# One small tile moved to another pool, two pads, and the result stored by halves in a two-layer PEER trunk

## The chip, the cores and the metric

The kernel runs on one core of one Trainium2 chip. Its engines are TensorE (PE in the rows; its weight loads are PEld), VectorE (DVE), ScalarE (ACT), GpSimd (POOL) and SyncE (SP), which issues most of the DMA transfers. The metric is the device time of one execution in microseconds (us), as the median of several runs.

## What is computed

The reference is a trunk of two layers over 512 tokens of 1024 channels, in float32. In each layer a mixing part is added to x and then a PEER part (product-key expert retrieval) is added. The PEER part matters most here:

```python
def peer_ffn(h, wq, keys, u, v):                      # u, v: 16384 experts x 1024
    q = (h @ wq).reshape(B, S, PEER_HEADS, 2, half)
    ...                                               # top 16 of the 16 x 16 best key pairs, 8 heads
    experts = e1 * PEER_NKEYS + e2
    gates = jax.nn.softmax(sc, axis=-1)
    def block(args):
        ht, et, gt = args
        act = jax.nn.gelu(jnp.einsum('td,ted->te', ht, u[et]), approximate=False)
        return jnp.einsum('te,ted->td', gt * act, v[et])
```

## The kernel before

The program is four parts one after the other: `mix_even`, `peer(0)`, `mix_odd`, `peer(1)`. Tokens are handled in four blocks of 128. In a PEER part block 0 gathers its experts' rows by indirect DMA (tile `gr`), and blocks 1 to 3 are computed densely over all 16384 experts, in 128 tiles of 128 experts.

**Split operands.** Each large float32 product is made of three fp32r matmuls: an operand is split into a high and a low part (`split`, L53 on ACT and L54 on DVE), and high x high, high x low and low x high are accumulated (`mm3`, L87 to L89; `v_sweep`, L1156). A weight tile comes by DMA as `raw` (four buffers) and is split into `whi` and `wlo` (three buffers each); these live in the pool `ws`. The transposed activations `hhi` and `hlo` live in the pool `hp`. In the rows a matmul reads `out<-moving,stationary`.

**The two stages of a PEER part.** The first stage (`u_step`, L87 to L89, `pu<-hhi,whi`) computes the activations of 128 experts for 384 tokens: stationary `whi`, moving `hhi`. The activation goes by way of `xact` to DRAM (`aside`), or stays in `act`. Meanwhile the gates of all experts are made (`big`, to DRAM as `G`). The second stage (`prepare` and `v_sweep`) loads gates (`gc`) and activations (`at`), multiplies them (L1096), splits the product into `wh` and `wl` (L1100, 128 x 384), and for each expert tile issues 18 matmuls of 512 columns (L1156, `acc<-whi,wh`): stationary a 128-column piece of `wh` or `wl`, moving a half of `whi` or `wlo`. Each stationary piece is used for two matmuls in a row, into two accumulators.

**Other matmuls of 512 columns.** `out_proj` (L221) is the output projection of both mixing parts, by the same lines: stationary the mixing result, moving `whi` and `wlo`. In `mix_even` the result lies in a `hhi`/`hlo` tile of the pool `hp`; in `mix_odd` it lies in `ohi` and `olo` of the pool `m1`. In `mix_odd` the first two weight tiles of the value projection are split into `vhi` and `vlo` of the pool `lead` (moving, against stationary `hhi`/`hlo`), the next two into `whi` and `wlo` by the same `sweep`. The forget gates use 16-column stationary pieces of `wfh` and `wfl` (`pf`, L685 to L687).

**Order.** The instructions are put in order by the framework's scheduler, engine by engine; SP issues its transfers in the program's order, each waiting for its own semaphores.

**Lines that the change touches.** `mix_even` (L291) allocates `gc0`, the first norm's gains, 128 x 8 float32, in the pool `np` for the whole program, and loads it ahead of the token blocks 1 to 3; `first_norm` reads it in L324 and L325. `np` lies before the pools of the parts, so all of these lie behind `gc0`. `odd_begin` (L635) opens `lead` on the right side of the memory; `mix_odd_body` (L659) has the tile `fb`; L1189 to L1192 add the accumulators to x; L1231 and L1232 store x.

Of the kernel before, what the change touches and what calls it, by code (L numbers as in the profile page):

```python
# [6 lines left out]
F32 = mybir.dt.float32  # L7
# [11 lines left out]
P = 128  # L19
D = 1024  # L20
T = 512
NB = T // P
KD = D // P
# [5 lines left out]
DB = (1, 2, 3)  # L29
# [18 lines left out]
class Trunk:  # L48
# [242 lines left out]
    def mix_even(self):  # L291
        nc, tc, A = self.nc, self.tc, self.A
        hT = self.new_hT()
        gc = self.np.tile([P, KD], F32, name="gc0")
        nc.sync.dma_start(gc, A["gain0"])
        for b in range(1, NB):
            nc.sync.dma_start(self.xb[b], A["x"][b * P:(b + 1) * P])

        self.early = [self.raw(A["w_in0"][i]) for i in (0, 4, 3, 7)]
        with tc.tile_pool(name="m0c", bufs=1) as sc:  # L300
            nc.sync.dma_start(self.cst[:, P:], A["consts"][:, P:])
            self.first_norm(gc, hT)
            self.mix_even_body(hT, sc)
# [331 lines left out]
    def odd_begin(self):  # L635


        nc, tc, A = self.nc, self.tc, self.A
        with tc.issue_after(self.last_gelu.ins), tc.issue_after(self.last_act.ins):
            nc.scalar.preload_act_table_set("natural_log_exp_and_others")  # L640
        hT = self.new_hT()
        norm = self.norm(2, NB)
        pool = tc.tile_pool(name="lead", bufs=2, side="right", reuse_waits="tile")
        start, rest = self.nat_parts(A["w_v1"][0], self.rows(hT), 2, eng=nc.gpsimd, pool=pool.__enter__())

        def close():
            pool.__exit__(None, None, None)
            norm[2]()

        self.odd = hT, rest, close  # L650
        return hT, norm, start
# [7 lines left out]
    def mix_odd_body(self, hT, sc, rest):  # L659
        nc, tc, A = self.nc, self.tc, self.A  # L660
        self.t2 = 4
        with tc.tile_pool(name="m1", bufs=1) as sp:
            pool = tc.tile_pool(name="m1b", bufs=2)
# [1 line left out]
            qkg = sc.tile([P, 2], F32, name="qkg")  # L665
            nc.sync.dma_start(qkg, A["qk_g"])
            nc.vector.tensor_scalar(qkg[:, 0:1], qkg[:, 0:1], 0.125, None, op0=ALU.mult)
            fb = sc.tile([16, 1], F32, name="fb")
            nc.sync.dma_start(fb, A["fgate_b"])
            nmask = sc.tile([P, P], BF16, name="nmask")  # L670
            nmf = sc.tile([P, P], F32, name="nmf")
# [263 lines left out]
    def peer_body(self, L, hT, h0, run, last, sp, sb):  # L935
        nc, tc, A = self.nc, self.tc, self.A
# [250 lines left out]
        for b in range(nd):  # L1187
            run(v_sweep, tail, b)
            for c in range(2):  # L1189
                xa = self.xb[DB[b]][:, c * 512:(c + 1) * 512]  # L1190
                with tc.issue_after(self.last_xs.ins) if L == 0 else nullcontext():
                    nc.vector.tensor_tensor(xa, xa, acc[b][c], op=ALU.add)  # L1192
            if L == 0:
                scale(DB[b])
                if b == 1:
                    run(put, 0, hN, True)
# [9 lines left out]
    def build(self, stop=4, first=0):  # L1206
        nc, tc, A = self.nc, self.tc, self.A
        with tc.tile_pool(name="const", bufs=1) as cp, tc.tile_pool(name="ws", bufs=1) as self.ws, \
                tc.tile_pool(name="hp", bufs=1) as self.hp, tc.tile_pool(name="np", bufs=1) as self.np, \
                tc.tile_pool(name="dp", bufs=2, space=DRAM) as self.dp, \  # L1210
                tc.tile_pool(name="ps", bufs=1, space=PSUM) as self.ps:
            self.nx = 0
            self.x0 = cp.tile([P, D], F32, name="x0")
            self.open_x()
            cst = cp.tile([P, 5 * P + T], F32, name="cst")
            nc.sync.dma_start(self.x0, A["x"][0:P])
            nc.sync.dma_start(cst[:, 0:P], A["consts"][:, 0:P])
            self.ident, self.iota, self.o512, self.o128, self.b64 = [cst[:, i * P:(i + 1) * P] for i in range(5)]
            self.tri = cst[:, 5 * P:]
            self.orow = A["consts"][0:1, 5 * P:]  # L1220
            sc = cp.tile([P, 2], F32, name="sc")
            self.last_gelu = self.last_act = nc.vector.memset(sc[:, 0:1], -0.5)
            nc.vector.memset(sc[:, 1:2], EPS)
            self.mhalf, self.epsc = sc[:, 0:1], sc[:, 1:2]
            self.steps = cp.tile([P, 2, TOPK, TOPK], BF16, name="steps")
            self.stf = cp.tile([P, 2, TOPK], F32, name="stf")
            self.cst, self.early = cst, []
            for i, f in enumerate((self.mix_even, lambda: self.peer(0), self.mix_odd, lambda: self.peer(1))):
                if first <= i < stop:
                    f()  # L1230
            for b in range(NB):  # L1231
                nc.sync.dma_start(self.out[b * P:(b + 1) * P], self.xb[b])  # L1232
            self.close_x()


# [79 lines left out]
```

## Time and profile before

| what | value |
|---|---|
| median of 3 runs (lowest to highest) | 3128.29 us (3126.55 to 3131.29) |
| profiled execution, its own time | 3129.1 us |
| its span | 3127.3 us |
| PE busy | 3090.1 us (99%) |
| DVE, ACT, POOL busy | 77%, 44%, 35% |
| moved by DMA | 786.63 MB, mean 252 GB/s |

The span is the time from the first to the last instruction; 1.8 us of the profiled execution lie around it. In the rows a matmul's own duration is modelled and overlaps the next one's, so a stream of matmuls is read by the starts, not by the durations.

### The profile page before, as it was taken

Reading aid. Unit: us, or ns where it says so; the run is one execution under the profiler, and the core shown is the slowest. Engines: PE = TensorE matmul, PEld = TensorE weight load, DVE = VectorE, ACT = ScalarE, POOL = GpSimd, SP = SyncE. Lnnn points to the kernel's source line nnn. Section 1 sums busy time; section 2 is a strip of 40 time slices with the busy share of each in tenths; the row PEclk is TensorE's granted clock in tenths of the full one; section 3 lists DMA queues with packets and bytes.
Section 4 is the critical chain, followed back from the end, with each engine's and each line's share of the span. In section 5 each row is a group of like instructions: output and inputs, shape, how many; then the busy total and the mean of one; then the engine's idle time right before and its main releaser. Section 6 shows DMA issues by size and latency. Waiting matters only on the chain.

```text
span 3127.3 us, 45688 instructions
## 1 busy us (share of the span) xinstructions
PE 3090.1 (99%) x15932; PEld 2682.5 (86%) x15932; DVE 2403.1 (77%) x4938; ACT 1385.3 (44%) x2222; POOL 1102.7 (35%) x800
## 2 busy tenths in 40 slices
PE   8999999999999999999999999999999999999999
PEld 6668999999999888888776669999999998888887
DVE  7765988888886888888646549998888867888886
ACT  4353334666664333333334433336666643333332
POOL 1210123996773222222100001219867742222220
PEclk9999999999999999999999999999999999999999
DMA  4103445999998999999421124449999998999995
GB/s 156 54 29 129 144 135 181 354 356 342 340 322 303 316 345 359 356 345 368 163 69 41 43 96 137 139 144 339 366 335 343 326 333 277 350 350 352 364 352 208
DMA packets 334201, 786.63 MB, mean 252 GB/s; under 512 B 26873, under 2 KB 181898, under 8 KB 327826
## 3 DMA queue, kind: packets, MB, share of 16 engines
q1 hardware_dynamic: 260242, 515.24, 47.2%
q0 software_dynamic: 73728, 268.47, 24.5%
q8 instruction: 125, 2.05, 0.3%
q14 instruction: 106, 0.87, 0.1%
HBM read 687.07 MB, written 96.47 MB: 251 GB/s over the span
## 4 chain that ended last, share of the span: by engine, by line
PE 91%; DMA 3%; DVE 3%; issue 1%; ACT 1%; POOL 1%; SPq 0%; DVEq 0%; POOLq 0%; ACTq 0%
PE acc L1156 34%; PE pu L87 10%; PE pu L88 10%; PE pu L89 10%; PE bank L87 5%; PE bank L88 5%; PE bank L89 5%; PE bank L1030 4%; DMA gr<-in_uN_dram,ids 3%; PE pc L376 1%; PE po L779 1%; PE bank L747 1%; PE bank L1058 1%; DVE wlo L54 1%; DVE gr L982 1%
## 5 line engine op out<-in xcount | busy, mean ns | idle before, releaser
L53 ACT ACTIVATE whi<-raw 128x1024 fp32r<-128x1024 f32 x602 | 637.2, 1059 | 1531.4 <-issue 666.1
L54 DVE TENSOR_TENSOR wlo<-raw,whi 128x1024 fp32r<-128x1024 f32 x565 | 693.3, 1227 | 362.0 <-ACT whi L53 361.2
L87 PE MATMUL pu<-hhi,whi 128*128 128x384 f32 x2048 | 699.7, 342 | 0.9 <-ACT hhi L122 0.9
L89 PE MATMUL pu<-hhi,wlo 128*128 128x384 f32 x2048 | 688.1, 336 | 2.2 <-DVE wlo L54 2.2
L88 PE MATMUL pu<-hlo,whi 128*128 128x384 f32 x2048 | 686.0, 335 | 0.3 <-DVE hlo L123 0.3
L991 POOL DMA_INDIRECT gr<-in_vF_dram,ids x256 | 275.6, 1076 | 749.2 <-DVE x L993 724.6
L1156 PE MATMUL acc<-whi,wh 128*128 128x512 f32 x1536 | 450.5, 396 | 0.0
L1156 PE MATMUL acc<-wlo,wh 128*128 128x512 f32 x1536 | 449.8, 395 | 0.0
L1156 PE MATMUL acc<-whi,wl 128*128 128x512 f32 x1536 | 448.2, 395 | 0.0
L980 POOL DMA_INDIRECT gr<-in_uN_dram,ids x256 | 350.9, 1371 | 245.4 <-DVE dots L982 149.2
L87 PEld LDWEIGHTS pu<-hhi,whi 128*128 128x128 f32 x2048 | 385.6, 188 | 2.6 <-ACT hhi L122 1.3
L89 PEld LDWEIGHTS pu<-hhi,wlo 128*128 128x128 f32 x2048 | 384.8, 188 | 3.0 <-DVE wlo L54 2.8
L88 PEld LDWEIGHTS pu<-hlo,whi 128*128 128x128 f32 x2048 | 385.4, 188 | 2.3 <-DVE hlo L123 1.0
L1156 PEld LDWEIGHTS acc<-whi,wl 128*128 128x128 f32 x1536 | 288.6, 188 | 69.9
L1156 PEld LDWEIGHTS acc<-wlo,wh 128*128 128x128 f32 x1536 | 288.6, 188 | 69.6
L1156 PEld LDWEIGHTS acc<-whi,wh 128*128 128x128 f32 x1536 | 288.5, 188 | 69.4
L1020 POOL TENSOR_SCALAR a<-cst,sT 128x128 f32<-128x128 f32 x192 | 326.6, 1701 | 14.4 <-PE bank L1030 8.6
L993 DVE SCALAR_TENSOR_TENSOR x<-gr,dots,x 128x1024 f32<-128x1024 f32 x256 | 327.4, 1279 | 0.0
L982 DVE CUSTOM_DVE_ANT_0 gr<-gr,h 128x1024 f32<-128x1024 f32 x256 | 308.3, 1223 | 24.2 <-DMA gr<-in_uN_dram,ids 24.1
L1017 DVE TENSOR_TENSOR a<-cst,sT 128x512 f32<-128x512 f32 x192 | 132.7, 691 | 126.6 <-PE bank L1030 121.4
L54 POOL TENSOR_TENSOR wlo<-raw,whi 128x1024 fp32r<-128x1024 f32 x37 | 93.9, 2538 | 374.5 <-ACT whi L53 366.5
L87 PE MATMUL bank<-hhi,whi 128*128 128x512 f32 x512 | 211.0, 413 | 1.5 <-ACT hhi L122 1.5
(267 smaller groups left out, 4093.0 us busy)
## 6 DMA issues: line engine op xcount, KB each, us to landing
raw<-in_uT_dram SPq DMA_DIRECT2D x256, 512.0 KB
raw<-in_vF_dram SPq DMA_DIRECT2D x256, 512.0 KB
G<-big SPq DMA_DIRECT2D x48, 1024.0 KB
gc<-G SPq DMA_DIRECT2D x32, 1536.0 KB
aside<-xact SPq DMA_DIRECT2D x208, 192.0 KB
at<-aside SPq DMA_DIRECT2D x104, 384.0 KB
raw<-in_w_in_dram SPq DMA_DIRECT2D x32, 512.0 KB
raw<-in_wq_dram SPq DMA_DIRECT2D x32, 512.0 KB
```

What stands on the lines that cost most here:

```text
L53: first = self.nc.scalar.activation(hi, raw, AF.Copy)
L54: self.last_lo = (eng or self.nc.vector).tensor_tensor(lo, raw, hi.bitcast(F32), op=ALU.subtract)
L87: mm(out, lh, rh, start=first, stop=False)
L88: mm(out, lh, rl, start=False, stop=False)
L89: return mm(out, ll, rh, start=False, stop=last)
L980: nc.gpsimd.indirect_dma_start(out=r, out_offset=None, in_=uN, in_offset=bass.IndirectOffsetOnAxis(ap=ids[:, s:s + 1], axis=0))
L982: return lambda: nc.vector.tensor_tensor_reduce(r, r, h0, 1.0, 0.0, ALU.mult, ALU.add, accum_out=dots[:, s:s + 1])
L991: nc.gpsimd.indirect_dma_start(out=r, out_offset=None, in_=vF, in_offset=bass.IndirectOffsetOnAxis(ap=ids[:, s:s + 1], axis=0))
L993: return lambda: nc.vector.scalar_tensor_tensor(self.x0, r, dots[:, s:s + 1], self.x0, op0=ALU.mult, op1=ALU.add)
L1017: nc.vector.tensor_tensor(a2, self.iota[:, None, :].to_broadcast([P, 4, P]), e2[:, :, None].to_broadcast([P, 4, P]), op=ALU.is_equal)
L1020: (nc.vector if t else nc.gpsimd).tensor_scalar(a1[:, t], self.iota, e1[:, t:t + 1], gate[:, t:t + 1], op0=ALU.is_equal, op1=ALU.mult)
L1156: mm = nc.tensor.matmul(acc[b][c], wt[:, s], vt[:, c], start=(n == 0 and wt is wh and vt is vh), stop=(n == NE1 - 1 and wt is wl))
```

## The change

The first norm's gains `gc0` become a tile of the pool `m0c`, which lives only as long as the first mixing part, and their load is written behind the loads of the token blocks. With `gc0` out of `np`, everything that is allocated behind `np` starts 32 bytes lower in each partition; inside the first mixing part `gc0` takes these 32 bytes again, so the tiles there stay where they were. Two pads move two places further: a tile of 64 bytes in `lead`, and `fb`, which grows from 4 to 96 bytes. At the end each half of a block is stored behind its own addition, as six transfers of 128 x 512, instead of three of 128 x 1024; block 0 keeps its store.

```diff
@@ mix_even
-        gc = self.np.tile([P, KD], F32, name="gc0")
-        nc.sync.dma_start(gc, A["gain0"])
         for b in range(1, NB):
             nc.sync.dma_start(self.xb[b], A["x"][b * P:(b + 1) * P])
-        self.early = [self.raw(A["w_in0"][i]) for i in (0, 4, 3, 7)]
         with tc.tile_pool(name="m0c", bufs=1) as sc:
+            gc = sc.tile([P, KD], F32, name="gc0")
+            nc.sync.dma_start(gc, A["gain0"])
+            self.early = [self.raw(A["w_in0"][i]) for i in (0, 4, 3, 7)]
@@ odd_begin
-        start, rest = self.nat_parts(A["w_v1"][0], self.rows(hT), 2, eng=nc.gpsimd, pool=pool.__enter__())
+        lead = pool.__enter__()
+        start, rest = self.nat_parts(A["w_v1"][0], self.rows(hT), 2, eng=nc.gpsimd, pool=lead)
+        lead.tile([P, 16], F32, name="pad", bufs=1)
@@ mix_odd_body
-            fb = sc.tile([16, 1], F32, name="fb")
+            fb = sc.tile([16, 24], F32, name="fb")[:, 0:1]
@@ peer_body
                     nc.vector.tensor_tensor(xa, xa, acc[b][c], op=ALU.add)
+                if L:
+                    nc.sync.dma_start(self.out[DB[b] * P:(DB[b] + 1) * P, c * 512:(c + 1) * 512], xa)
@@ build
-            for b in range(NB):
-                nc.sync.dma_start(self.out[b * P:(b + 1) * P], self.xb[b])
+            nc.sync.dma_start(self.out[0:P], self.x0)
```

Where the tiles start in a partition, by the two built programs (bytes; the remainder is by 256; the buffers of one tile name lie multiples of 256 bytes apart, and so do the pieces of them that the matmuls use, except in `wfh`):

| tile | before | remainder | changed | remainder |
|---|---|---|---|---|
| `whi`, `wlo` (first buffers) | 42784, 55072 | 32 | 42784, 55072 | 32 |
| `hhi`, `hlo` | 67360, 83744 | 32 | 67360, 83744 | 32 |
| `wh`, `wl` | 163904, 168512 | 64 | 163872, 168480 | 32 |
| `ohi`, `olo` | 127872, 144256 | 128 | 127904, 144288 | 160 |
| `vhi`, `vlo` | 184288, 192480 | 224 | 184224, 192416 | 160 |
| `wfh`, piece k at + 64 k | 106112 | 128 (k = 0) | 106144 | 160 (k = 0) |
| `gc`, `at`, `xact`, `act0`, `h0` | 173120, 197696, 159296, 122432, 104512 | 64 | 32 bytes lower | 32 |
| `raw`, `gr`, `upad`, `x0` | | | unchanged | |

On PE, DVE, ACT and POOL every instruction stands where it stood. On SP two places differ. The first is the program's start: `x_72` is token block 0, `x` blocks 1 to 3, `gc_87` and `gc_93` are the gains, `raw` the first weight tiles. Before:

```order
L1216 DMA x_72<-in_x_dram 128x1024
L1217 DMA cst<-in_consts_dram 128x128
L295 DMA gc_87<-in_gain_dram 128x8
L297 DMA x<-in_x_dram 128x1024 x3
L59 DMA raw<-in_w_in_dram 128x1024 x4
```

and changed:

```order
L1220 DMA x_72<-in_x_dram 128x1024
L1221 DMA cst<-in_consts_dram 128x128
L295 DMA x<-in_x_dram 128x1024 x3
L298 DMA gc_93<-in_gain_dram 128x8
L59 DMA raw<-in_w_in_dram 128x1024 x4
```

The load of the gains has moved behind three loads of 512 KB. The second place is SP's end, the last weight tiles and the stores, before:

```order
L1000 DMA x<-kept 128x1024 x3
L1085 DMA at<-aside 128x2x384
L1232 DMA out_dram<-x_72 128x1024
L59 DMA raw<-in_vF_dram 128x1024 x3
L1232 DMA out_dram<-x 128x1024 x3
```

and changed:

```order
L1002 DMA x<-kept 128x1024 x3
L1087 DMA at<-aside 128x2x384
L1235 DMA out_dram<-x_72 128x1024
L59 DMA raw<-in_vF_dram 128x1024 x3
L1196 DMA out_dram<-x 128x512 x6
```

Three stores of 512 KB have become six of 256 KB; nothing stands behind them on SP.

## Rows read from the trace of the kernel before

**Rows 1.** The page's head and PE's row: busy, share, instructions.
```profile
span 3127.3 us, 45688 instructions
...
PE 3090.1 (99%) x15932; PEld 2682.5 (86%) x15932; DVE 2403.1 (77%) x4938; ACT 1385.3 (44%) x2222; POOL 1102.7 (35%) x800
```
**Rows 2.** Chain of work, second PEER stages (first cut at 1500): start, us, what.
```profile
1005.21 494.89 PE acc L1156 x2121
...
2586.66 535.74 PE acc L1156 x2296
```
**Rows 3.** Group of L1156: xcount | busy, mean ns; group of L87: xcount, ns min/median/max.
```profile
L1156 PE MATMUL acc<-whi,wh 128*128 128x512 f32 x1536 | 450.5, 396 | 0.0
...
L87 PE MATMUL bank<-whi,ohi x64: 391/398/790, 1783.0 to 1854.1; 128*128 128x512 f32 x64
```
**Rows 4.** Timeline of PE, output projection of mix_even: start, us, operation.
```profile
237.83 0.39 PE L87 MATMUL bank<-whi,hhi 128*128 128x512 f32 x1
...
245.99 0.39 PE L87 MATMUL bank<-whi,hhi 128*128 128x512 f32 x1
```
**Rows 5.** Timeline of PE, output projection of mix_odd.
```profile
1838.34 0.40 PE L89 MATMUL bank<-whi,olo 128*128 128x512 f32 x1
...
1847.47 0.39 PE L89 MATMUL bank<-whi,olo 128*128 128x512 f32 x1
```
**Rows 6.** Timeline of PE, value projection of mix_odd, two kinds of weight tile.
```profile
1556.71 0.39 PE L89 MATMUL bank<-vhi,hlo 128*128 128x512 f32 x1
...
1558.81 0.40 PE L89 MATMUL bank<-vhi,hlo 128*128 128x512 f32 x1
...
1564.33 0.39 PE L87 MATMUL bank<-whi,hhi 128*128 128x512 f32 x1
...
1565.92 0.39 PE L88 MATMUL bank<-wlo,hhi 128*128 128x512 f32 x1
```
**Rows 7.** Timeline of PE, forget gates, starts of pieces k = 1, 2, 3, 6, 7.
```profile
1559.50 0.40 PE L87 MATMUL bank<-hhi,wfh 128*16 128x512 f32 x1
...
1560.20 0.39 PE L87 MATMUL bank<-hhi,wfh 128*16 128x512 f32 x1
...
1560.88 0.40 PE L87 MATMUL bank<-hhi,wfh 128*16 128x512 f32 x1
...
1562.96 0.39 PE L87 MATMUL bank<-hhi,wfh 128*16 128x512 f32 x1
...
1563.64 0.40 PE L87 MATMUL bank<-hhi,wfh 128*16 128x512 f32 x1
```
**Rows 8.** Stretches: PE, PEld, DVE, ACT, POOL busy (x), PEclk, DMA share, GB/s.
```profile
1000.00:1500.00 500.00, 500.00 (x2150) 403.32 (x2150) 408.32 (x484) 177.71 (x242) 130.21 (x123) 1.00 0.97 339
...
1100.00:1108.40 8.40, 8.40 (x37) 6.76 (x36) 7.56 (x11) 2.95 (x4) 3.56 (x3) 1.00 1.08 351
1108.40:1116.80 8.40, 8.40 (x37) 6.76 (x36) 6.98 (x9) 2.95 (x4) 2.12 (x3) 1.00 1.03 402
```
**Rows 9.** Line L384, taps of the convolution: ns min/median/max.
```profile
L384 DVE SCALAR_TENSOR_TENSOR y<-upad,cw,y x79: 730/743/1779, 34.9 to 120.9; 128x512 f32<-128x512 f32 x79
```
**Rows 10.** Timeline of the program's start, SP's queue and ACT.
```profile
1.64 0.43 SPq L295 DMA_DIRECT2D gc<-in_gain_dram  x1
...
12.21 1.06 ACT L53 ACTIVATE whi<-raw 128x1024 fp32r<-128x1024 f32 x1 [0.23 <-DMA raw<-in_w_in_dram]
```
**Rows 11.** Stretches at the program's end, columns as in rows 8.
```profile
3124.00:3125.00 1.00, 0.00 (x0) 0.00 (x0) 0.00 (x0) 0.00 (x0) 0.00 (x0) 1.00 0.47 188
3125.00:3126.00 1.00, 0.00 (x0) 0.00 (x0) 0.00 (x0) 0.00 (x0) 0.00 (x0) 1.00 0.84 336
```
**Rows 12.** Timeline of PE, a query projection of peer(1) right after first-stage matmuls.
```profile
1867.36 0.39 PE L88 MATMUL bank<-hlo,whi 128*128 128x512 f32 x1
...
1869.21 0.39 PE L87 MATMUL bank<-hhi,whi 128*128 128x512 f32 x1
...
1877.60 0.39 PE L89 MATMUL bank<-hhi,wlo 128*128 128x512 f32 x1
```

## The prediction

> **What bounds the kernel now.** I began with the page's head and the busy line [rows 1]: PE is busy 3090.1 of 3127.3 us. At most some 37 us lie in PE's idle time; a larger gain must come from PE's own stream running faster, and what is saved on another engine is lost unless PE waited for it. The chain of waits, in order of time, says where nothing but PE decides: the second stage of each PEER part is one single piece, 2121 matmuls in 494.89 us in the first (cut at 1500) and 2296 in 535.74 us in the second [rows 2]. No wait is left inside them, and both make 233.3 ns per matmul. The groups by form give their number: three groups of 1536, so 4608 [rows 3], 1075 us or 34% of the span. The mean of one in that view (396 ns) is no guide, since matmuls overlap; the starts are.
>
> So I compared the starts of the same matmul (128 x 128 stationary, 512 columns moving, fp32r) in other places of the timeline:
> - Output projection of `mix_even`: 36 starts in 8.16 us, 226.7 ns each [rows 4].
> - Output projection of `mix_odd`, the same lines of code: 39 starts in 9.13 us, 234.1 ns [rows 5].
> - Value projection of `mix_odd` with moving `vhi`/`vlo`: 9 starts in 2.10 us, 233.3 ns; some 6 us later, the same loop with moving `whi`/`wlo`: 7 starts in 1.59 us, 227.1 ns [rows 6].
>
> There are two spacings, about 7 ns apart, for one shape. The same code runs at both, so it isn't the instruction pattern alone. What goes along with the spacing is the place of the operands, in the table of start addresses: where stationary and moving both leave 32 by 256, the matmuls start 226.7 ns apart; where one of them leaves 64 (`wh`), 128 (`ohi`) or 224 (`vhi`) against 32, they start 233.3 to 234.1 apart. That the remainder by 256 counts, and nothing longer, I take from the forget gates, whose stationary pieces step by 64 bytes: the three matmuls of k = 1 (remainder 192) take 0.70 us, those of k = 2 and of k = 6, which lie 256 bytes apart and both leave 0, take 0.68 [rows 7]. Rows are rounded to 0.01, so this is weak support, and there 0 does as well as 32. The trace doesn't show why the place should count.
>
> **The change part by part.**
>
> *Place of `wh` and `wl`.* They go from remainder 64 to 32, the remainder of the moving `whi` and `wlo`, the pairing of rows 4. I take 226.7 ns for all of them: 4608 x (233.3 - 226.7) = **30.7 us off**, all of it on the path, since the two pieces of rows 2 hold no wait. Ends of the range: 0 (they stay at 233.3) and 30.7 (no row of this shape is faster in a steady stream).
>
> *Cover for that.* The second stage of 1000 to 1500 must then be fed in 486 us instead of 500. DVE is busy 408 us of it, so it keeps 78 us; ACT and POOL are far off [rows 8]. DMA is nearest: 339 GB/s at a busy share of 0.97, which would have to be 349. One stretch of 8.4 us moves 402, its neighbour, at a share of 1.08, only 351 [rows 8]. Since the rate reaches 402 and the mean needed is 349, I cost this at nothing; without that cover it is the second rival. The Trainium skill ("DMA: Bandwidth & Descriptors", section "Where 436 GB/s comes from") puts the HBM limit of a core at about 358 GB/s; the stretch at 402 is above it, so the trace doesn't bear it out as a ceiling, and by it the stage would still fit, with little to spare.
>
> *Place of `ohi`/`olo` and `vhi`/`vlo`.* From 128 and 224 to 160, against 32. No row shows a 128-column tile at 160. Three groups of 64 matmuls on the projection [rows 3] at 234.1 could fall to 226.7 (1.4 us), 48 on `vhi` and `vlo` (two tiles, two halves, four blocks, three products) from 233.3 likewise (0.3 us). I take half, **0.8 off**, ends 0 and 1.7: 160 is 128 beyond 32, and half a period may or may not do.
>
> *All other shifted tiles* (`gc`, `at`, `act`, `h0` and so on, from 64 to 32; in `mix_odd` up by 32). DVE doesn't mind: 79 taps read `upad` at 31 different 4-byte offsets, minimum 730, median 743 ns [rows 9]. Zero; and what DVE would lose lies under PE, by the 78 us above. The first stages' matmuls use `whi`, `wlo`, `hhi` and `hlo` alone, which don't move: zero.
>
> *The gains' load.* Three token loads are issued 0.43 us earlier, the gains behind them [rows 10]. The first norm could be up to 0.43 us earlier; but ACT's split of the second weight tile at 12.21 waits for its own transfer [rows 10], whose issue doesn't move, and the first use of the gains stands behind it on ACT. **0.1 off**, ends 0 and 0.43. The gains' 4 KB arrive behind three loads of 512 KB; if they were later than that split, the first projection would wait for them.
>
> *The stores.* The last store of 512 KB fills 3124 to 3126: 188 and 336 GB/s for one us each [rows 11]. With 256 KB left behind the last addition, at 336 GB/s, 0.78 us less remain at most; the first half goes out during the second addition. **0.6 off**, ends 0 and 0.78. On SP only other stores stand behind, and no engine waits for them.
>
> The sum, against the profiled execution's own 3129.1 us (span 3127.3 and 1.8 around it): 3129.1 - 30.7 - 0.8 - 0.1 - 0.6 = 3096.9. That execution is 0.8 above the median of the runs, 3128.3; against the median it is **3096.1 us**, 1.0% faster.
>
> **The rivals.**
>
> *The spacing stays.* For it: the second stage has a pattern that no row shows at 226.7, each stationary piece used twice running, two moving halves into two accumulators. And the spacing is a state that a stream settles into rather than a fixed price: a query projection with all operands at 32 begins with 8 starts in 1.85 us, 231 ns each, and goes on with 37 in 8.39, 226.8 ns [rows 12]; the second stage never settled in 2296. Against it: rows 4 to 6, where the same code changes its spacing with the place. It leaves 0.1 to 1.5 us of gain: 3127.5. The Trainium skill ("SBUF — State Buffer", section "A bandwidth-pool intuition that's wrong (but worth ruling out)") gives TensorE a second, independent read port for weight loads and knows contention only where engines share a port; by it the place of the stationary operand could not matter, and the time would be this rival's. Rows 4 and 5 speak against it.
>
> *DMA takes over.* The stage runs at 226.7 until the gate loads, at 351 GB/s, hold back the weight tiles; half of the gain is given back: 3096 + 15 = 3111 or so. For it: the share of 1.08; against it: 402 GB/s right behind.
>
> *Slower: a worse pairing.* The second stages settle at a spacing above 233.3, since the place counts and the new pairing is not what I take it for. `ohi` at 234.1 shows that pairings differ upwards too. Each ns costs 4.6 us, so it is slower beyond 0.2% from 1.4 ns (6.3 us) up; one step of 6.7 ns more would give 3128 + 31 = 3159. Against it: no steady row of this shape above 234.1, and `wh` joins a pairing that rows 4 show.
>
> **How the numbers follow.** About 0.2% (6.3 us) is what a measurement of this kernel can tell from no change: 3122 to 3134.6 is the same. Chances: forecast 0.76, DMA 0.08, spacing stays 0.12, worse pairing 0.04. The first two are both faster: 0.84; same 0.12; slower 0.04. The forecast's own range: 3092 (0 for nothing, all ends at their far side, and 2 us for runs, which lie within -1.7 and +3.0 of their median) to 3101 (place of `ohi` and the stores worth nothing, beginnings at 231 ns, and 3 us for runs). With the DMA case it reaches to 3113; that holds a little over 0.8.
>
> **What would show it.** The two pieces of the chain: 2296 matmuls in about 520.5 us instead of 535.7, starts 226.7 ns apart; if they stay at 233.3, the reading of rows 4 to 6 is wrong, or right for those patterns only. First stages and first mixing part: unchanged lengths. `mix_odd`: starts of `ohi` at 226.7 or 234. The second stage's DMA near 349 GB/s and no PE idle time inside; gaps that end on `raw` would show the DMA case. The last transfers about 0.6 us shorter behind the last addition. Wrong altogether would be a change of time with the spacing unchanged.

## The result and the profile after

The changed kernel takes 3100.15 us (median of 4 runs, 3098.18 to 3100.8), the kernel before 3129.34 beside it (4 runs, 3126.55 to 3131.29): a ratio of 0.9906, 95% interval 0.9889 to 0.9923. It is faster, and the time lies in the range of the prediction (3092 to 3113), 4 us above the forecast of 3096.1. In a second series it took 3097.95 (4 runs), ratio 0.9905 (0.9888 to 0.9922). The profiled execution after has 3100.8 us of its own and a span of 3099.0; the one before had 3129.1 and 3127.3.

The page's head and the busy line, which answer to [rows 1]:

```profile
span 3099.0 us, 45694 instructions
...
PE 3058.8 (99%) x15932; PEld 2681.2 (87%) x15932; DVE 2401.9 (78%) x4938; ACT 1386.9 (45%) x2222; POOL 1109.5 (36%) x800
```

PE has the same 15932 matmuls and is busy 31.3 us less; the span is only 28.3 us shorter. So PE's stream runs faster, as forecast, and 3.0 us of PE's idle time have been added (40.2 us instead of 37.2). Both are followed below.

The chain of waits of after, the pieces of the second stages (start, us, what), which answer to [rows 2]; the first one here is not cut at 1500:

```profile
1005.23 505.89 PE acc L1158 x2232
...
2573.83 520.48 PE acc L1158 x2296
```

L1158 is L1156 of before. The second piece makes 520.48 / 2296 = 226.7 ns per matmul instead of 233.3, and 520.5 us were forecast. The first makes 505.89 / 2232 = 226.7; the same piece of before, uncut, is

```profile
1005.21 520.68 PE acc L1156 x2232
```

The two pieces are 14.79 and 15.26 us shorter, 30.05 together, and they still hold no wait. The stretch 1000 to 1500 of after, columns as in [rows 8]:

```profile
1000.00:1500.00 500.00, 500.00 (x2213) 414.60 (x2212) 416.46 (x494) 182.75 (x248) 132.34 (x123) 1.00 0.98 346
```

PE does 2213 matmuls in it instead of 2150, is never idle, and the DMA moves 346 GB/s (349 were forecast) at a share of 0.98. The rival in which the DMA takes over did not come. The granted clock is 1.00 in both kernels, the 2.4 GHz level; the spacing is no matter of the clock.

### The profile page after: what moved, and what is told of

The parts are those of the page before. It is cut to its first block, busy times and chain, and to the rows that moved or that the text cites. A ratio compares the mean times of both kernels' runs of the same rounds, so it can differ in the third digit from the quotient of the medians.

```text
span 3099.0 us, 45694 instructions
## 1 busy us (share of the span) xinstructions
PE 3058.8 (99%) x15932; PEld 2681.2 (87%) x15932; DVE 2401.9 (78%) x4938; ACT 1386.9 (45%) x2222; POOL 1109.5 (36%) x800
## 4 chain that ended last, share of the span: by engine, by line
PE 91%; DVE 3%; DMA 2%; issue 2%; ACT 1%; POOL 1%; SPq 0%; DVEq 0%; POOLq 0%; ACTq 0%
PE acc L1158 33%; PE pu L88 10%; PE pu L87 10%; PE pu L89 10%; PE bank L87 6%; PE bank L89 5%; PE bank L88 5%; PE bank L1032 4%; DMA gr<-in_uN_dram,ids 2%; PE pc L376 1%; PE po L781 1%; PE bank L749 1%; PE bank L1060 1%; DVE gr L984 1%; DVE wlo L54 1%
## 5 line engine op out<-in xcount | busy, mean ns | idle before, releaser
L87 PE MATMUL pu<-hhi,whi 128*128 128x384 f32 x2048 | 698.7, 341 | 1.2 <-ACT hhi L122 1.2
L1158 PE MATMUL acc<-whi,wh 128*128 128x512 f32 x1536 | 439.9, 389 | 0.0
L1158 PE MATMUL acc<-wlo,wh 128*128 128x512 f32 x1536 | 439.2, 389 | 0.0
L1158 PE MATMUL acc<-whi,wl 128*128 128x512 f32 x1536 | 437.3, 389 | 0.0
L87 PEld LDWEIGHTS pu<-hhi,whi 128*128 128x128 f32 x2048 | 385.7, 188 | 2.7 <-ACT hhi L122 1.4
L1158 PEld LDWEIGHTS acc<-whi,wl 128*128 128x128 f32 x1536 | 288.3, 188 | 59.9
L1158 PEld LDWEIGHTS acc<-wlo,wh 128*128 128x128 f32 x1536 | 288.3, 188 | 59.9
L1158 PEld LDWEIGHTS acc<-whi,wh 128*128 128x128 f32 x1536 | 288.2, 188 | 59.5
L1022 POOL TENSOR_SCALAR a<-cst,sT 128x128 f32<-128x128 f32 x192 | 334.6, 1743 | 14.3 <-PE bank L1032 6.3
L87 PE MATMUL bank<-hhi,whi 128*128 128x512 f32 x512 | 211.0, 413 | 1.4 <-ACT hhi L122 1.4
```

Source lines behind the costliest of these rows:

```text
L87: mm(out, lh, rh, start=first, stop=False)
L1022: (nc.vector if t else nc.gpsimd).tensor_scalar(a1[:, t], self.iota, e1[:, t:t + 1], gate[:, t:t + 1], op0=ALU.is_equal, op1=ALU.mult)
L1158: mm = nc.tensor.matmul(acc[b][c], wt[:, s], vt[:, c], start=(n == 0 and wt is wh and vt is vh), stop=(n == NE1 - 1 and wt is wl))
```

## The experiments

### Only the place of wh and wl

The kernel before with a pad of 224 bytes, and nothing else of the change:

```diff
                 wb, vb = wpool.__enter__(), vpool.__enter__()
+                wb.tile([P, 56], F32, name="pad", bufs=1)
```

> The kernel before with one edit: a 224-byte pad ahead of wh and wl, which brings them (and gc and at) to remainder 32 by 256; the gains' load, ohi, vhi, the first stages' tiles and the stores stay as before. Theory (the place of wh against whi alone makes the gain): both second stages at 226.7 ns per matmul (2296 in about 520.5 us), time about 30 us below before, near 3098 to 3099; ohi stays at 234.1, the program's start and the second layer's first stage are as in before, so it is 0 to 4 us faster than the changed kernel if the later start and the 3 us lost in that first stage come from the other edits. Rival (the gain needs the other moved tiles, as act, gc0 or the pools behind np): 233.3 ns stay, 3128. If the 3 us in the first stage are noise, this kernel shows them or not as it likes; if they come from the moved a1 and a2 tiles, the stage ends as in before.

Measured: 3099.8 us (4 runs), ratio 0.9906 (0.9889 to 0.9922), the same as the whole change. Its chain of waits, second layer:

```profile
2574.19 520.48 PE acc L1157 x2296
```

The same 520.48 us. The gain needs this one place and none of the other edits. The 0 to 4 us by which this kernel was to be faster than the changed one did not come: in the same series the changed kernel took 3097.95.

### The place of wh and wl taken back

The changed kernel with a pad of 32 bytes, which brings them back to 64:

```diff
                 wb, vb = wpool.__enter__(), vpool.__enter__()
+                wb.tile([P, 8], F32, name="pad", bufs=1)
```

> The changed kernel with a pad of 32 bytes ahead of wh and wl: they are back at remainder 64, all else of the change stays. Theory (place of wh against whi): second stages back at 233.3 ns, 2296 in 535.7 us, about 3130. Rival (the other tiles that moved bring the gain, or the stores do): 226.7 ns, 3100.

Measured: 3126.68 us (one run). Its chain, second layer:

```profile
2584.44 535.74 PE acc L1159 x2296
```

That is the 535.74 us of [rows 2], with all other edits in place. Together with the run before, the gain is undone and done by the place of these two tiles alone.

### Everything at 64

The changed kernel with 32 bytes ahead of the constants, so that the whole left side of the memory moves, `whi` and `wlo` with `wh` and `wl`:

```diff
+            cp.tile([P, 8], F32, name="pad")
             cst = cp.tile([P, 5 * P + T], F32, name="cst")
```

> The changed kernel with everything that lies on the memory's left side 32 bytes higher: whi, wlo, hhi, hlo, wh and wl all leave 64 by 256 (ohi 192, vhi stays at 160). Theory (what counts is that both operands leave the same remainder): second stages at 226.7 ns, as in the changed kernel, 3098 to 3100. Rival (the place of wh itself counts: 64 is a bad place for a stationary operand, or for any): 233.3 ns, about 3129, and the first stages and projections, now at 64 too, slow down with it.

Measured: 3095.27 us (one run). Its chain, second layer:

```profile
2568.28 520.48 PE acc L1158 x2296
```

Both operands at 64: 226.7 ns. Against `whi` at 32 the same 64 gave 233.3. So 64 is not a bad place by itself; it is the distance between the two that counts. The pads of the two runs before moved the tiles `gc` and `at` together with `wh`; here these two lie at 64 as in the kernel before, so they have no part in the gain.

### The other distances

Three kernels with another pad at the same place, a different one in each layer:

```diff
                 wb, vb = wpool.__enter__(), vpool.__enter__()
+                wb.tile([P, (56, 24)[L]], F32, name="pad", bufs=1)
```

The pads are 56 and 24 words for remainders 0 and 128, 16 and 32 for 96 and 160, 40 and 48 for 192 and 224.

> The changed kernel with wh and wl at remainder 0 in the first layer and 128 in the second, against whi at 32. Theory in its strict form (same remainder by 256 or slow): 233.3 ns in both stages, about 3129. Rival (remainder by 64 or 128 decides, or small distances are as good): 0 is 32 away as 64 is, so 233.3; 128 is 96 away; a stage that shows 226.7 falls out of the strict form.

> The changed kernel with wh and wl at remainder 96 in the first layer and 160 in the second. Theory in its strict form (same remainder by 256): 233.3 ns in both, about 3129. Rivals: a period of 64 gives 226.7 in both, 3099; a period of 128 gives 226.7 in the second alone, about 3114 (15 us of the 30 kept).

> The changed kernel with wh and wl at remainder 192 in the first layer and 224 in the second. Theory in its strict form: 233.3 ns in both, about 3129. Rival with a period of 64: 224 gives 226.7, 192 does not, about 3114. A third value of the spacing in a stage would say that the distance sets it step by step.

Measured: 3130.51, 3122.69 and 3119.94 us (one run each). Chain of waits, first layer (cut at 1500) and second layer, for remainders 0 and 128:

```profile
1005.21 494.90 PE acc L1159 x2121
...
2586.03 537.93 PE acc L1159 x2296
```

for 96 and 160:

```profile
1004.95 495.13 PE acc L1159 x2122
...
2582.63 533.56 PE acc L1159 x2296
```

and for 192 and 224:

```profile
1004.92 495.13 PE acc L1159 x2122
...
2587.90 525.54 PE acc L1159 x2296
```

Length by count, with `whi` and `wlo` at 32:

| `wh`, `wl` leave | beyond `whi` | ns per matmul |
|---|---|---|
| 32 | 0 | 226.7 |
| 64 (before) | 32 | 233.3 |
| 96 | 64 | 233.3 |
| 128 | 96 | 234.3 |
| 160 | 128 | 232.4 |
| 192 | 160 | 233.3 |
| 224 | 192 | 228.9 |
| 0 | 224 | 233.3 |

The distances 0 and 32 were measured in both layers, each of the others in one layer only. Of the eight places one alone gives 226.7. Periods of 64 and 128, the rivals in the expectations, fall: at 96 and 160 both stages should have been at 226.7 for the one, and the second for the other. The strict form of the theory ("same remainder, or 233.3") falls too: there are values in between, 228.9 above all. That nothing longer than 256 counts can be read from the table of addresses: `wh` at 163872 and `whi` at 42784 lie 473 x 256 bytes apart, an odd multiple, and run at 226.7. With the pad of 224 bytes on the kernel before, `wh` starts at 164128, an even multiple (474), and they run at 226.7 too.

### One of the two tiles misplaced

```diff
             wh = wb.tile([P, TD], F32R, name="wh")
+            if n == 0:
+                wb.tile([P, (8, 56)[L]], F32, name="pad2", bufs=1)
             wl = wb.tile([P, TD], F32R, name="wl")
...
                 wb, vb = wpool.__enter__(), vpool.__enter__()
+                if L:
+                    wb.tile([P, 8], F32, name="pad", bufs=1)
```

> The changed kernel with wh and wl apart by one pad between them: in the first layer wl alone is at remainder 64 and wh at 32, in the second wh alone is at 64 and wl at 32; whi and wlo stay at 32. One matmul in three has wl as its stationary operand. Theory with a price for each matmul whose stationary operand leaves another remainder: the first layer's second stage at 226.7 + 6.6/3 = 228.9 ns, the second layer's at 226.7 + 2 x 6.6/3 = 231.1, about 3100 + 5 + 10 = 3115; the longer starts stand at the matmuls with the tile that moved, or at their neighbours. Rival (one state for the whole stream, which any misplaced operand brings about): 233.3 in both, about 3129. A second rival (wh alone counts, or the first piece of a tile): 226.7 in one and 233.3 in the other, 3114.

Measured: 3120.42 us (one run). Chain of waits, first layer (`wl` at 64) and second (`wh` at 64):

```profile
1006.71 514.79 PE acc L1162 x2232
...
2581.38 532.51 PE acc L1162 x2296
```

230.6 and 231.9 ns, where a price for each misplaced matmul gave 228.9 and 231.1, one state for the whole stream 233.3 and 233.3, and the second rival 226.7 and 233.3. Over whole stages none of the three fits. Two stretches of the first layer's stage (columns as in [rows 8]) differ:

```profile
1010.00:1110.00 100.00, 100.00 (x433) 80.95 (x432) 83.76 (x101) 35.80 (x49) 28.08 (x26) 1.00 0.93 310
...
1310.00:1410.00 100.00, 100.00 (x438) 81.83 (x437) 83.17 (x99) 36.27 (x50) 28.04 (x27) 1.00 1.02 363
```

With the same tiles at the same places, 433 matmuls fall in one stretch of 100 us and 438 in a later one. What differs is the order in which the scheduler put them. Timeline of PE in the first stretch:

```profile
1040.60 0.62 PE L1162 MATMUL acc<-whi,wl 128*128 128x512 f32 x2
1041.06 0.63 PE L1162 MATMUL acc<-whi,wh 128*128 128x512 f32 x2
1041.53 0.62 PE L1162 MATMUL acc<-wlo,wh 128*128 128x512 f32 x2
1041.98 0.63 PE L1162 MATMUL acc<-whi,wl 128*128 128x512 f32 x2
...
1054.51 0.63 PE L1162 MATMUL acc<-whi,wl 128*128 128x512 f32 x2
```

and in the later one:

```profile
1340.94 1.56 PE L1162 MATMUL acc<-whi,wl 128*128 128x512 f32 x6
1342.34 1.53 PE L1162 MATMUL acc<-whi,wh 128*128 128x512 f32 x6
1343.70 1.53 PE L1162 MATMUL acc<-wlo,wh 128*128 128x512 f32 x6
1345.07 1.56 PE L1162 MATMUL acc<-whi,wl 128*128 128x512 f32 x6
```

In the first, the places change with every second or fourth matmul, and 60 starts take 13.91 us, 231.8 ns each. In the later one six with the misplaced `wl` take 1.40 us (233 ns each), and the next twelve, with `wh` in place, 2.73 (227.5). There the price for each misplaced matmul nearly holds: 18 starts in 4.13 us, 229.4 ns, where the theory gave 228.9. Where the places change more often, the stream as a whole pays more than that price. [rows 12] had shown that a stream needs some matmuls until its spacing comes down.

### PE left alone

The changed kernel with `wh` at 64 in the first layer and 32 in the second; tiles 2 to 111 of the second stage use the weights and products of tiles 0 and 1 again:

```diff
+QUIET = 112
...
-            if m % EC == 0 and m < NE1:
+            if m % EC == 0 and m < NE1 and not 0 < m < QUIET:
...
+            if 2 <= n < QUIET:
+                lo, t = held[n % 2]
+                return lo, (n, *t[1:])
...
-            return lo, (n, vh, vl, wh, wl)
+            held.append((lo, (n, vh, vl, wh, wl)))
+            return held[-1]
```

> The changed kernel with wh and wl at remainder 64 in the first layer and 32 in the second, and with the second stage's tiles 2 to 111 left out: their matmuls take the weights and the split products of tiles 0 and 1 again, so that for most of the stage no weight is loaded or split and PE works nearly alone (its output is not the trunk's). Theory (the spacing comes from PE's own two reads, stationary and moving): 233.3 ns in the first layer and 226.7 in the second, also where DVE, ACT and the DMA are silent. Rival (the spacing at 64 comes from others that read or write next to PE, such as the splits into whi and wh or the weight transfers): 226.7 in both layers while they are silent, and 233.3 only in the stretches in which they work. Time near 3115 by the theory, near 3100 by the rival; a start or an end of the stage that waits more than before may move it by some us.

Measured: 3116.01 us (one run). A stretch of each stage, columns as in [rows 8]:

```profile
1300.00:1400.00 100.00, 100.00 (x430) 80.49 (x429) 0.00 (x0) 0.00 (x0) 0.00 (x0) 1.00 0.00 0
2870.00:2970.00 100.00, 100.00 (x443) 82.83 (x442) 0.00 (x0) 0.00 (x0) 0.00 (x0) 1.00 0.00 1
```

In these two stretches DVE, ACT and POOL do nothing, the DMA moves next to nothing, and 430 matmuls of PE fall in 100 us with `wh` at 64 and 443 at 32. The chain has both stages:

```profile
1004.90 495.13 PE acc L1167 x2122
...
2589.13 520.48 PE acc L1167 x2296
```

495.13 / 2122 = 233.3 and 520.48 / 2296 = 226.7, as with everybody at work. So no other engine and no transfer takes part. PE makes the difference between its own operands; by what step of its reading them, no run shows.

### The activations misplaced

The changed kernel with `hhi` and `hlo` at 64, and all behind them where it was by 256:

```diff
             cst = cp.tile([P, 5 * P + T], F32, name="cst")
+            self.hp.tile([P, 8], F32, name="pad", bufs=1)
+            self.np.tile([P, 56], F32, name="pad", bufs=1)
```

> The changed kernel with hhi and hlo, the transposed activations, at remainder 64 (a pad of 32 bytes ahead of them and one of 224 behind, so that all that follows keeps its remainder); whi, wlo, wh and wl stay at 32. Now the moving operand of the first stages (384 columns) and of the query projections, and the stationary one of the other projections, are misplaced, and the second stages are not. Theory (it holds for every stream of fp32r matmuls, on either side): first-stage matmuls go from 173 ns starts to about 180, 6144 of them, 41 us, and some 1970 matmuls of 512 columns in the projections from 226.7 to 233.3, 13 us; with what stands in streams too short to settle 40 to 55 us, so near 3145; the second stages stay at 226.7. Rival (it needs 512 columns, or the place of the stationary operand alone counts): the first stages stay at 173, and only the projections with stationary hhi lose, some 3 us, near 3101.

Measured: 3107.82 us (one run), between the theory's 3145 and the rival's 3101, and 8 to 10 us above the changed kernel. The timeline of PE, output projection of `mix_even` (stationary `hhi`, [rows 4] of before):

```profile
242.61 0.40 PE L87 MATMUL bank<-whi,hhi 128*128 128x512 f32 x1
...
246.81 0.40 PE L87 MATMUL bank<-whi,hhi 128*128 128x512 f32 x1
```

18 starts in 4.20 us, 233.3 ns; [rows 4] had 226.7. A query projection of the second layer, in which `hhi` moves and `whi` is stationary:

```profile
1910.35 0.40 PE L89 MATMUL bank<-hhi,wlo 128*128 128x512 f32 x1
...
1920.85 0.40 PE L89 MATMUL bank<-hhi,wlo 128*128 128x512 f32 x1
```

The same one in the changed kernel:

```profile
1904.56 0.39 PE L89 MATMUL bank<-hhi,wlo 128*128 128x512 f32 x1
...
1912.72 0.39 PE L89 MATMUL bank<-hhi,wlo 128*128 128x512 f32 x1
```

45 starts in 10.50 us, 233.3 ns, against 36 in 8.16, 226.7 ns, behind nine slower ones. With 512 columns the moving side pays as the stationary side does, and the 8 to 10 us answer to the 13 that the theory had put for the projections. With 384 columns it hardly does. The first stage by form (nanoseconds: min/median/max), in this kernel and in the changed one:

```profile
L87 PE MATMUL pu<-hhi,whi x2048: 331/336/686, 276.4 to 2580.2; 128*128 128x384 f32 x187
```

```profile
L87 PE MATMUL pu<-hhi,whi x2048: 332/334/687, 273.5 to 2573.1; 128*128 128x384 f32 x187
```

The medians differ by 2 ns, and a stretch of the first stage from 750 to 950 holds 1286 matmuls in this kernel and 1284 in the changed one:

```profile
750.00:950.00 200.00, 200.00 (x1286) 200.00 (x1285) 161.84 (x286) 127.65 (x215) 147.97 (x100) 1.00 0.93 331
```

So the expectation was half wrong: it holds for either side, but not for every stream. In this stretch PEld is busy all of the 200 us, where in the second stage it was busy 415 of 500. That may be why 7 ns elsewhere don't show here; no run tested it.

### mix_odd at the same remainder, and the gains first

The changed kernel with `ohi`, `olo`, `vhi`, `vlo` and `wfh` at 32 as well, and the gains' load back at its old place; beside it the changed kernel itself once more:

```diff
+            gc = sc.tile([P, KD], F32, name="gc0")
+            nc.sync.dma_start(gc, A["gain0"])
             for b in range(1, NB):
                 nc.sync.dma_start(self.xb[b], A["x"][b * P:(b + 1) * P])
-            gc = sc.tile([P, KD], F32, name="gc0")
-            nc.sync.dma_start(gc, A["gain0"])
...
-        lead.tile([P, 16], F32, name="pad", bufs=1)
+        lead.tile([P, 48], F32, name="pad", bufs=1)
...
-            fb = sc.tile([16, 24], F32, name="fb")[:, 0:1]
+            fb = sc.tile([16, 56], F32, name="fb")[:, 0:1]
```

> The changed kernel with ohi, olo, vhi, vlo and wfh at remainder 32 (longer pads) and the gains' load back ahead of the token blocks. Theory (same remainder gives 226.7; the later start comes from the order of the loads): starts of the output projection of mix_odd at 226.7 instead of 232 to 234, about 1.3 us; first projection about 1 us earlier; together 1.5 to 2.5 us below the changed kernel, near 3098. Rival (128 beyond is as good as it gets, and the start has its own spread): no difference, 3100.

> The changed kernel once more, on the same chip as the other three, so that small differences can be read: 3100 by its own times. The later start (first projection matmul near 18.97 us instead of 18.01) should show again if it comes from the moved load; the second layer's first stage loses 3 us again if that comes from the moved tiles, and doesn't if it is chance.

Measured: 3097.51 us (3097.34 to 3098.07, 4 runs) against 3097.95 (3097.45 to 3100.5) for the changed kernel; ratios to before 0.9902 (0.9886 to 0.9919) and 0.9905 (0.9888 to 0.9922). No difference that these runs can tell, where 1.5 to 2.5 us were expected. The two parts are nevertheless to be seen in the traces. The output projection of `mix_odd`, the 39 starts of [rows 5], in the changed kernel (`ohi` at 160):

```profile
1823.11 0.40 PE L89 MATMUL bank<-whi,olo 128*128 128x512 f32 x1
...
1832.18 0.40 PE L89 MATMUL bank<-whi,olo 128*128 128x512 f32 x1
```

and with `ohi` at 32:

```profile
1821.43 0.40 PE L89 MATMUL bank<-whi,olo 128*128 128x512 f32 x1
...
1823.99 0.39 PE L88 MATMUL bank<-wlo,ohi 128*128 128x512 f32 x1
...
1830.33 0.40 PE L89 MATMUL bank<-whi,olo 128*128 128x512 f32 x1
```

9.13 us before, 9.07 at 160 (232.6 ns), 8.90 at 32: there 11 starts in 2.56 us, 233 ns, until the stream settles, and then 28 in 6.34, 226.4 ns. `mix_odd` has short streams, and much of each is over before it has settled.

The program's start, timeline of ACT (the second block's square, then the split of the second weight tile, [rows 10]), in the changed kernel:

```profile
7.45 1.06 ACT L315 ACTIVATE xs<-x 128x1024 f32<-128x1024 f32 x1 [1.91 <-DMA x<-in_x_dram]
...
13.34 1.06 ACT L53 ACTIVATE whi<-raw 128x1024 fp32r<-128x1024 f32 x1 [0.23 <-DMA raw<-in_w_in_dram]
```

and before:

```profile
6.96 1.06 ACT L315 ACTIVATE xs<-x 128x1024 f32<-128x1024 f32 x1 [1.46 <-DMA x<-in_x_dram]
```

The load of token block 1 is issued 0.47 us earlier after the change (at 1.64 instead of 2.11 us), and its data are used 0.49 later. Over all executions shown here, the first projection matmul starts at 18.01 to 18.58 us where the gains are loaded first (three kernels, mean 18.3) and at 18.50 to 19.54 where they are loaded behind (ten, mean 19.0). The edges overlap, but the order that was meant to help goes with a start some 0.7 us later. No engine waited for the gains themselves: in the changed kernel ACT first uses them at 14.30 us, right behind the split that starts at 13.34. Why the blocks land later was not settled.

The 3 us of idle time: stretch 2128 to 2226 of the second layer's first stage, columns as in [rows 8], in the changed kernel's two profiled executions, the first execution first:

```profile
2128.00:2226.00 98.00, 93.01 (x586) 91.36 (x586) 82.84 (x145) 59.62 (x100) 89.17 (x53) 1.00 0.97 359
```

```profile
2128.00:2226.00 98.00, 95.28 (x606) 94.00 (x605) 84.29 (x148) 60.44 (x101) 90.71 (x54) 1.00 0.99 362
```

PE is busy 93.0 us of it in one and 95.3 in the other, for the same program; before it was 95.4, and 95.6 in the stretch 15 us later, where the same work lies. In the waits of PE for this stretch, the matmuls wait for POOL's `a` 4.6 us in the first and 2.0 in the second. The same program shows both, so it is a difference between executions. From its first matmul to the second stage's first, this first stage takes 725.9 us before, and 728.4 and 725.1 in the two executions of the changed kernel.

## Why the prediction was right, and where it was not

- **Place of `wh` and `wl`: right, in size too.** 30.7 us were forecast (from the unrounded 233.33 and 226.67; the factors as printed give 30.4), 30.05 are shown by the two pieces of the chain, which hold 4528 of the 4608 matmuls. The reading of [rows 4 to 6] was that operands at the same remainder run at 226.7; the runs with everything at 64 and with PE left alone bear it out for this place, and show that it is PE's own. The rival by which the spacing stays fell. So did the result that the prediction drew from the Trainium skill ("SBUF — State Buffer", section "A bandwidth-pool intuition that's wrong (but worth ruling out)"): with a read port of its own for weights, the place of the stationary operand could not matter; 430 against 443 matmuls in 100 us with nothing else at work say that it does.
- **The forget gates [rows 7] were no support.** In them 0 did as well as 32; in the second stage 0 ran at 233.3. What they were quoted for, a period of 256, came out right by other runs.
- **`ohi`, `olo`, `vhi`, `vlo`: half was too much.** 0.8 us were put for 160. It measures 232.4 in the second stages and 232.6 in the projection, so 192 x (234.1 - 232.6) = 0.3 us. Half a period is nearly as bad as the rest. Even 226.7 there would have given less than the 1.4 of the bound, for the streams are too short to settle.
- **The gains' load: wrong sign.** 0.1 off was forecast with ends 0 and 0.43; about 0.7 was lost. The step that failed is the one that let the data come earlier because the issue does. The issue moved by 0.47 us, not by the 0.43 read from [rows 10].
- **The stores: 0.2 instead of 0.6.** From the start of the last block's two additions to the span's end it is 4.88 us before, 4.90 with the place alone and whole stores, 4.66 after. The last stretches of after, columns as in [rows 8] and beside [rows 11]:

```profile
3094.00:3095.00 1.00, 0.52 (x3) 0.10 (x1) 0.67 (x2) 0.00 (x0) 0.00 (x0) 1.00 0.00 0
3095.00:3096.00 1.00, 0.00 (x0) 0.00 (x0) 0.62 (x2) 0.00 (x0) 0.00 (x0) 1.00 0.12 45
3096.00:3097.00 1.00, 0.00 (x0) 0.00 (x0) 0.00 (x0) 0.00 (x0) 0.00 (x0) 1.00 1.03 381
3097.00:3098.00 1.00, 0.00 (x0) 0.00 (x0) 0.00 (x0) 0.00 (x0) 0.00 (x0) 1.00 0.27 98
```

  45 + 381 + 98 = 524 KB move in these three us, as much as the 188 + 336 of [rows 11]. The step "the first half goes out during the second addition" failed: the additions end at 3095.62, and the transfers begin only behind them:

```profile
3095.60:3095.80 0.20, 0.00 (x0) 0.00 (x0) 0.02 (x1) 0.00 (x0) 0.00 (x0) 1.00 0.00 0
3095.80:3096.00 0.20, 0.00 (x0) 0.00 (x0) 0.00 (x0) 0.00 (x0) 0.00 (x0) 1.00 0.62 225
```

  Even so the bytes are through earlier, about 3.0 us after the start of the two additions instead of 3.5 before, close to the 0.6 that was forecast. But from the last byte to the end of the span it is 1.7 us with halves and 1.4 with whole stores, so that only 0.2 of it reaches the end. Why that tail is longer, no run shows.
- **First stages: unforeseen.** The second layer's moved by 3.3 us between two executions of the changed kernel, more than all the small terms together. In the profiled execution after, 1.3 us were lost up to the first layer's first stage and 2.5 in the second layer's, and 1.2 were gained in the first layer's: 2.5 of the 4 us between 3096.1 and 3100.15. What such stages add or take from one execution to the next is luck, for the forecast as against it.
- **Worse pairings exist**, but only just: 234.3 with `wh` at remainder 128. The step of 6.7 ns more that the slower rival priced was not found.

## What to carry to other kernels

A PE-bound stream of 512-column fp32r matmuls, long enough to settle, is worth a look at where its two operands start: bring all stationary and moving tiles to the same remainder by 256 bytes (a mixture gave less than its share here), and compare starts, since the durations of single matmuls (389 to 396 ns) overlap and are not the spacing. A small tile allocated early, or a pad, moves all pools behind it, so an edit that has nothing to do with PE can gain or lose time, 1% here. Below some 3 us, differences of one execution to another in waiting stages hide what an edit does; read such terms in their own stretch.

## What the runs showed that was not expected

- The spacing by distance (0 to 224 in steps of 32): 226.7, 233.3, 233.3, 234.3, 232.4, 233.3, 228.9, 233.3 ns. It is neither two values nor a smooth curve; what brings 192 nearest to 0 stays open.
- With one of the two tiles misplaced the order counts: 433 matmuls in 100 us where the places change every few matmuls, 438 where at least six of a kind follow each other.
- The first stage's 384-column matmuls don't show it: 1286 and 1284 in 200 us with the moving operand at 64 and at 32.
